# State space phase: x scaled by 1/rms as it is turned, B loaded ahead of w_in, u and z copied out by ScalarE, drive of the states behind two projections

## Chip, cores, metric

One core of a Trainium2 chip. The metric is the device time of one execution in microseconds (us), median of three runs. PE is TensorE, DVE VectorE, ACT ScalarE, POOL GpSimd, SP SyncE (it issues the DMAs here).

## What is computed

x is 256 tokens by 1024 columns. Two layers follow: an S5 mixer and an attention mixer, then two blocks of feed forward and hybrid mixer. The change touches the S5 mixer alone:

```python
def rms_norm(x, g):
    y = xf * lax.rsqrt(jnp.mean(xf * xf, axis=-1, keepdims=True) + NORM_EPS)
    return (y * g).astype(x.dtype)

def s5_mixer(h, w_in, a_re, a_im, log_dt, b_re, b_im, c_re, c_im, d_skip, w_glu, b_glu, w_out):
    proj = h @ w_in
    u, z = proj[..., :SSM_WIDTH], proj[..., SSM_WIDTH:]
    ...   # dt, ab = exp(a*dt), f = (ab - 1)/a, all complex; bu = B u per group of 16 channels
    ...   # s[t] = ab * s[t-1] + f * bu[t], by an associative scan over 256 tokens
    y = Re(C s) + d_skip * uf
    y = jax.nn.gelu(y)
    y = y * jax.nn.sigmoid(y @ w_glu + b_glu)
    y = y * jax.nn.silu(z)
    return y @ w_out
```

There are 64 groups of 16 channels with 64 complex states each.

## The kernel before

All engines run the program in the order in which it is written (a manual schedule), so the order of the source lines in `ssm` is the order on each engine; SP issues loads in their written order, and a load waits until its buffer is free.

Tiling. Channels lie on partitions, 8 blocks of 128 (`KC`). Tokens are cut into 64 chunks (`J`) of 4 (`L`). Two groups share a partition axis of 128 states, so there are 32 pairs (`NPR`). Within a chunk the work is matrix products: `vt` (B times powers of a, turned) carries u into the state increment of a chunk (`drive`), `kt` carries u of a chunk to y of the same chunk (`within`), `cp` (C times powers of a) reads states into y (`read`). Between chunks the states `S` are scanned on DVE in levels: `pre4` and `pre8` join chunks in twos and fours, `chain` takes 16 steps in a row over the fours, `post8` and `post4` fill in the rest. `drive(0)` and `drive(1)` each make half of the pairs; `settle` copies them from PSUM to S, one half on ACT and one on DVE; p4[0], p4[1], p8[0], p8[1] are the levels of the first half of the pairs, p4[2], p4[3], p8[2], p8[3] those of the second.

Projection. x is turned by 16 PE transposes (L772), ACT copies it out times the gain g (L779) to `xg`, and `proj(s)` (L790) makes 256 of the 2048 columns of w_in: s = 0 to 3 are u, 4 to 7 are z. 1/rms of a token isn't in xg: `norm()` finds it on DVE, PE spreads it over the partitions (L339), DVE copies it to `R` (rstd, L1154), and `evac_u` and `gate` on DVE multiply it in as they copy u and z out of PSUM with tokens regrouped as (t, j):

```python
    def evac_u(s):
        for m in range(2):
            V.tensor_tensor(u[:, 2 * s + m], perm(us[s][:, m]), perm(R), op=ALU.mult)
```

Parameters. `powers()` on DVE makes the powers of a from a_re, a_im and log_dt; `cmul` is a complex product of B or C (`raw`, tile `bc`) with one of them; `spread` (ACT, L976) lays a result out as `bx` (for B) or `cp` (for C); `turn_c` turns C on PE (L951) and ACT copies it back (L956); `turn_b` turns bx (L994), ACT copies it to vt (L997). `kernels` (L1062) makes `kps` on PE, `turn_k` (L1069) copies it turned to `kt`. `rest1` (L2092, L2094) turns bias rows on PE (`rows`) and copies them on DVE (`cols`).

The order around the change is: turns of x, proj(0); powers; B products woven with norm(); proj(1), proj(2); u(0), u(1), u(2) copied out; proj(3) woven with turn_b; drive(0) between its halves; p4[0], p4[1], p8[0]; u(3); kernels; drive(1); proj(4), proj(5); then DVE's p4[2] to p8[3]; turn_k woven with the first steps of chain; rest1; proj(6), proj(7); within; chain woven with gate(4), gate(5); post levels with four reads; then the GLU products with w_glu (L1261).

Of the kernel before, what the change touches and what calls it, by code (L numbers as in the profile page):

```python
# [18 lines left out]
P = 128  # L19
# [684 lines left out]
L = 4  # L704
# [4 lines left out]
def ssm(K, x, g, gcol, w_in, a_re, a_im, log_dt, b_re, b_im, c_re, c_im, d_skip, w_glu, rest0, rest1, rest2, w_out, follow):  # L709
# [21 lines left out]
    nc.sync.dma_start(h[:, 1], x[P:T])  # L731
    w0 = K.wp.tile([P, KC, 256], F32, tag="raw", name=K.name("raw"), bufs=3)
# [35 lines left out]
    xg = K.e([P, KC, T], "xg")  # L768
    xps = [K.psum("acc" if 0 < k < 3 else "ps", [P, 2, 2, P], "xp") for k in range(4)]
    for t in range(2):  # L770
        for k in range(KC):
            nc.tensor.transpose(xps[k // 2][:, k % 2, t], h[:, t, k * P:(k + 1) * P], K.ident)  # L772
        if t == 0:
            gp = K.psum("acc", [P, 2 * KC], "gp")
            nc.tensor.transpose(gp, g16, K.ident[:2 * KC, :2 * KC])
            nc.scalar.copy(gcol.rearrange("p l m -> p (l m)"), gp)
    xps = [x.rearrange("p i t c -> p i (t c)") for x in xps]
    for k in range(KC):
        nc.scalar.activation(xg[:, k], xps[k // 2][:, k % 2], AF.Copy, scale=gcol[:, 0, k:k + 1])  # L779
# [23 lines left out]

    run(proj(0))
# [79 lines left out]
    def powers():  # L884
        run(expm1(dt, t2))
        V.tensor_copy(pr[:, 0:2], pt)
        stt(dt, em, 1.0, t2, ALU.add, ALU.mult)
        tt(mag, lr, dt)
        tt(th, li, dt)
        for _ in zip_longest(magnitude(), trig()):  # L890
            pass
        tt(t1, t5, sn)
        tt(t2, sn, sn)
        tt(ai, t1, mag)
        stt(cm, t2, -2.0, mag, ALU.mult, ALU.mult)
        tt(ar, mag, cm, ALU.add)
# [82 lines left out]
    def perm(ap):  # L979
        return ap.rearrange("p (j t) -> p t j", t=L)  # L980
# [56 lines left out]
    def pre4(b):  # L1037
        return level(b, 1, slice(2, None, 2), slice(1, None, 2))
# [93 lines left out]
    wr, wh, wl = [], [], []  # L1132
    load()
    spread(lambda b: bx[b][:, :, 3], bp[3])
    nc.scalar.copy(cin[:, :, :, 1], cin[:, :, :, 0])
    nm = norm()
    run(weave(cmul(bp[2], bp[3], ar, ai), nm, 3))
    run(nm)
    run(proj(1))
    load()  # L1140
    rp = K.rows(stat[0], 2)
    R = K.ap.tile([P, T], F32, tag="rstd", name=K.name("rstd"), bufs=2)
    spread(lambda b: bx[b][:, :, 2], bp[2])
    run(cmul(bp[1], bp[2], ar, ai))
    spread(lambda b: bx[b][:, :, 1], bp[1])
    evacs = [turn_c(0, 0), turn_c(0, 4), turn_c(1, 0)]
    run(proj(2))
    for f in evacs:
        f()
    evacs = turn_c(1, 4)  # L1150
    run(cmul(bp[0], bp[1], ar, ai))
    spread(lambda b: bx[b][:, :, 0], bp[0])
    evacs()
    V.tensor_copy(R, rp)  # L1154
    evac_u(0)
    evac_u(1)
    factors()
    squarings()
    load()
    evac_u(2)  # L1160
# [8 lines left out]
    p3 = proj(3)  # L1169
    cp = [K.wp.tile([P, 2, L, 8, 2 * CH], F32, tag="wlo", name=K.name("cp")) for _ in range(4)]  # L1170

    def later(t):
        run(cmul(nxt, cur, ar, nai1))
        spread(lambda b: cp[b][:, :, t], nxt)
        return nxt, cur

# [5 lines left out]
    for m in range(4):  # L1182
        run(turn_b(m))
        run(p3, 2)
    cur, nxt = later(0)
    cur, nxt = later(1)
# [23 lines left out]
    skip = K.t([P, KC, 2 * CH], "skip")  # L1210
    V.tensor_tensor(skip, K.eye32[:, None, :].broadcast_to([P, KC, 2 * CH]),
                    dsk[:, :, None].broadcast_to([P, KC, 2 * CH]), op=ALU.mult)
    kt = K.e([P, KC, L, 2 * CH], "kt")
# [12 lines left out]
    for s in (4, 5):  # L1226
        run(weave(gate(s), ch))
# [16 lines left out]
    for s in (6, 7):  # L1244
        run(gate(s))
# [6 lines left out]
    for s in range(4, 8):  # L1252
        silu(s)
# [916 lines left out]
```

## Time and profile before

| | us |
|---|---|
| median of 3 runs (1393.80 to 1394.67) | 1394.28 |
| the profiled execution, its own time | 1394.2 |
| its span in the profile | 1392.1 |
| PE busy, share of the span | 1360.4, 98% |
| DVE busy | 1101.1, 79% |
| ACT busy | 817.5, 59% |
| first GLU product, the end of the stretch that the change touches | 125.96 |

Times in the profile are us from the span's start. In a row of the timeline the first number is the start, the second the time to the end of the group, then engine, line, operation, tiles written and read, shapes, and how many; in square brackets is how long the engine stood idle before and what ended that. An fp32 matmul counts as two PE instructions, a transpose as one. PE's ends are modelled; the distance from start to start is the surer measure.

### The profile page before, as it was taken

Reading aid. Unit: us, or ns where it says so; the run is one execution under the profiler, and the core shown is the slowest. Engines: PE = TensorE matmul, PEld = TensorE weight load, DVE = VectorE, ACT = ScalarE, POOL = GpSimd, SP = SyncE. Lnnn points to the kernel's source line nnn. Section 1 sums busy time; section 2 is a strip of 40 time slices with the busy share of each in tenths; the row PEclk is TensorE's granted clock in tenths of the full one; section 3 lists DMA queues with packets and bytes.
Section 4 is the critical chain, followed back from the end, with each engine's and each line's share of the span. In section 5 each row is a group of like instructions: output and inputs, shape, how many; then the busy total and the mean of one; then the engine's idle time right before and its main releaser. Section 6 shows DMA issues by size and latency. Waiting matters only on the chain. (4 is left out here: it accounts for less than half of the span.)

```text
span 1392.1 us, 21232 instructions
## 1 busy us (share of the span) xinstructions
PE 1360.4 (98%) x8205; PEld 1148.8 (83%) x8205; DVE 1101.1 (79%) x1801; ACT 817.5 (59%) x1589; POOL 27.4 (2%) x35
## 2 busy tenths in 40 slices
PE   8988999999999999999999999999999999999996
PEld 7877888987888899887878888788899887878885
DVE  8889788678996589777799747998469987698954
ACT  6524667665765484565676546666457564656642
POOL 0003100000000000000000000000000000000000
PEclk9999999999999999999999999999999999999998
DMA  8233655366637444455844656365535445747350
GB/s 217 63 112 119 207 172 170 123 189 234 222 111 241 150 155 159 152 165 168 272 137 166 198 188 222 125 236 182 199 128 187 138 163 177 225 150 259 119 183 30
DMA packets 181348, 237.17 MB, mean 170 GB/s; under 512 B 16952, under 2 KB 140144, under 8 KB 181248
## 3 DMA queue, kind: packets, MB, share of 16 engines
q1 hardware_dynamic: 180160, 233.47, 51.5%
q0 software_dynamic: 672, 1.81, 0.4%
q8 instruction: 64, 1.05, 0.3%
q10 hardware_dynamic: 416, 0.55, 0.1%
q14 instruction: 36, 0.29, 0.1%
HBM read 234.76 MB, written 1.05 MB: 169 GB/s over the span
## 5 line engine op out<-in xcount | busy, mean ns | idle before, releaser
L191 ACT CAST whi<-raw 128x512 fp32r<-128x512 f32 x688 | 379.2, 620 | 137.5 <-PE p L289 87.3
L203 DVE TENSOR_TENSOR wlo<-raw,whi 128x1024 fp32r<-128x1024 f32 x344 | 407.4, 1217 | 7.8 <-ACT whi L191 7.4
L287 PE MATMUL p<-whi,xghi 128*128 128x512 f32 x800 | 320.5, 401 | 0.0
L289 PE MATMUL p<-whi,xglo 128*128 128x512 f32 x800 | 312.5, 391 | 0.0
L288 PE MATMUL p<-wlo,xghi 128*128 128x512 f32 x800 | 311.8, 390 | 0.0
L289 PEld LDWEIGHTS p<-whi,xglo 128*128 128x128 f32 x800 | 150.1, 188 | 32.4
L288 PEld LDWEIGHTS p<-wlo,xghi 128*128 128x128 f32 x800 | 150.6, 188 | 28.7
L287 PEld LDWEIGHTS p<-whi,xghi 128*128 128x128 f32 x800 | 150.4, 188 | 28.6
L191 ACT CAST whi<-quad 128x512 fp32r<-128x512 f32 x192 | 106.5, 618 | 60.7 <-DVE quad L168 27.8
L287 PE MATMUL acc<-whi,hh 128*128 128x512 f32 x352 | 141.7, 402 | 0.0
L288 PE MATMUL acc<-wlo,hh 128*128 128x512 f32 x352 | 138.7, 394 | 0.1
L289 PE MATMUL acc<-whi,hh 128*128 128x512 f32 x352 | 138.1, 392 | 0.0
L203 DVE TENSOR_TENSOR wlo<-quad,whi 128x1024 fp32r<-128x1024 f32 x96 | 114.3, 1217 | 0.0
L506 DVE SCALAR_TENSOR_TENSOR hid<-p,col,hid 128x256 f32<-128x256 f32 x64 | 30.8, 481 | 75.5 <-ACT hid L505 75.1
L288 PEld LDWEIGHTS acc<-wlo,hh 128*128 128x128 f32 x352 | 66.2, 188 | 15.7 <-DVE wlo L203 3.8
L289 PEld LDWEIGHTS acc<-whi,hh 128*128 128x128 f32 x352 | 66.1, 188 | 15.4 <-DVE hh L301 1.7
L287 PEld LDWEIGHTS acc<-whi,hh 128*128 128x128 f32 x352 | 66.1, 188 | 13.7 <-ACT hh L300 1.6
L287 PE MATMUL g<-xghi,whi 128*128 128x256 f32 x256 | 73.8, 288 | 0.0
L289 PE MATMUL g<-xghi,wlo 128*128 128x256 f32 x256 | 72.4, 283 | 0.0
L288 PE MATMUL g<-xglo,whi 128*128 128x256 f32 x256 | 72.4, 283 | 0.0
L301 DVE TENSOR_TENSOR hh<-tph,hh 128x512 fp32r<-128x512 f32 x44 | 30.4, 690 | 49.6 <-ACT hh L300 49.3
L790 PE MATMUL g<-xg,raw 128*128 128x256 f32 x256 | 60.3, 392 | 4.6 <-DVE kt L1069 3.6
(375 smaller groups left out, 2248.6 us busy)
## 6 DMA issues: line engine op xcount, KB each, us to landing
raw<-in_ffn_w_down_dram SPq DMA_DIRECT2D x44, 1024.0 KB, 5.0
raw<-in_w_in_dram SPq DMA_DIRECT2D x36, 1024.0 KB, 5.1
raw<-in_ffn_w_gate_dram SPq DMA_DIRECT2D x56, 512.0 KB, 4.1
raw<-in_ffn_w_up_dram SPq DMA_DIRECT2D x56, 512.0 KB, 5.1
raw<-in_attn_w_in_dram SPq DMA_DIRECT2D x16, 1024.0 KB, 5.6
quad<-in_ffn_w_gate_dram SPq DMA_DIRECT2D x32, 512.0 KB, 8.8
quad<-in_ffn_w_up_dram SPq DMA_DIRECT2D x32, 512.0 KB, 8.8
raw<-in_w_out_dram SPq DMA_DIRECT2D x8, 1024.0 KB, 5.3
```

What stands on the lines that cost most here:

```text
L191: self.nc.scalar.copy(hf[:, sl], raw[:, sl])
L203: self.nc.vector.tensor_tensor(out, raw, hi.bitcast(F32), op=ALU.subtract)
L287: nc.tensor.matmul(out, ah, bh, start=start, stop=False, skip_group_check=more)
L288: nc.tensor.matmul(out, ah, bl, start=False, stop=False, skip_group_check=more)
L289: nc.tensor.matmul(out, al, bh, start=False, stop=stop, skip_group_check=more)
L301: self.nc.vector.tensor_tensor(lo, x, hi.bitcast(F32), op=ALU.subtract)
L506: V.scalar_tensor_tensor(hid[j, t], s[:, 256:512], norm.col05[:, t:t + 1], a, op0=ALU.mult, op1=ALU.mult)
L790: nc.tensor.matmul(us[s][:, m], ws[s][:, k, m * P:(m + 1) * P], xg[:, k], start=k == 0, stop=k == KC - 1)
```

## The change

x is turned by products with a diagonal matrix `dg` that holds 1/rms, so xg already has it; R, its spread and its copy are gone. u and z (4, 5) are copied out by ACT without a product, z (6, 7) goes through silu straight from PSUM. norm() stands inside powers() from its seventh turn on. B is loaded ahead of w0. proj(0) stands behind powers, C's turns behind proj(0) and proj(1), turn_b(0) to (3) and drive(0) behind these two; proj(2) and proj(3) follow drive(0) whole. turn_k, skip and the settling of the second half stand right behind drive(1), p8[1] ahead of it, the last spread of cp behind it. The chain is woven with nothing.

```diff
+    raw = K.e([P, 2, 2, NPR, CH], "bc")
+    for i, b in enumerate((b_re, b_im)):
+        nc.sync.dma_start(raw[:, 0, i], ...)
     w0 = ...
-    for t in range(2):
-        for k in range(KC):
-            nc.tensor.transpose(xps[k // 2][:, k % 2, t], h[:, t, k * P:(k + 1) * P], K.ident)
...
-    run(proj(0))
...
-        for _ in zip_longest(magnitude(), trig()):
-            pass
+        nm = norm()
+        for i, _ in enumerate(zip_longest(magnitude(), trig())):
+            if i >= 6:
+                next(nm, None)
+        run(nm)
...
     def evac_u(s):
-        for m in range(2):
-            V.tensor_tensor(u[:, 2 * s + m], perm(us[s][:, m]), perm(R), op=ALU.mult)
+        nc.scalar.copy(u[:, 2 * s:2 * s + 2], us[s].rearrange("p m (j t) -> p m t j", t=L))
...
     def gate(s):
-        for m in range(2):
-            V.tensor_tensor(z[:, 2 * (s - 4) + m], perm(us[s][:, m]), perm(R), op=ALU.mult)
-            yield
+        nc.scalar.copy(z[:, 2 * (s - 4):2 * (s - 4) + 2], us[s].rearrange("p m (j t) -> p m t j", t=L))
...
+    spread(lambda b: bx[b][:, :, 3], bp[3])
+    for t in range(2):
+        V.tensor_scalar(dg[:, t], K.ident, stat[0][:, t:t + 1], None, op0=ALU.mult)
...
+    for k in range(KC):
+        for t in range(2):
+            nc.tensor.matmul(xps[k // 2][:, k % 2, t], h[:, t, k * P:(k + 1) * P], dg[:, t], start=True, stop=True)
+        nc.scalar.activation(xg[:, k], xps[k // 2][:, k % 2].rearrange("p t c -> p (t c)"), AF.Copy,
+                             scale=gcol[:, 0, k:k + 1])
     load()
+    run(cmul(bp[2], bp[3], ar, ai))
+    run(proj(0))
...
+    evac_u(1)
+    for m in range(4):
+        run(turn_b(m))
+        if m == 0:
+            for f in evacs:
+                f()
     factors()
     squarings()
...
+    cur, nxt = later()
+    vq = drive(0)
+    laid(0)
+    cur, nxt = later()
+    settled(0, vq)
+    laid(1)
+    run(proj(2))
     load()
+    evac_u(2)
     run(p4[0])
     run(weave(p4[1], p8[0]))
+    run(p8[1])
+    run(proj(3))
     evac_u(3)
+    for m in range(4, KC):
+        run(turn_b(m))
     kps = [kernels(hf) for hf in range(2)]
+    cur, nxt = later()
+    laid(2)
+    later()
     vq = drive(1)
+    for hf in range(2):
+        run(turn_k(hf))
     settled(1, vq)
+    laid(3)
     run(proj(4))
-    run(weave(p4[2], p8[1]))
+    run(p4[2])
     run(weave(p4[3], p8[2]))
     run(p8[3])
     run(proj(5))
     ch = chain()
-    for hf in range(2):
-        run(weave(turn_k(hf), ch))
     b_glu = rest1(rowsin)
     run(proj(6))
...
     for s in (4, 5):
-        run(weave(gate(s), ch))
+        gate(s)
     run(ch)
```

On PE from the parameters' transposes (pt) on, before: xp is x turned, gp the gains, g a projection.

```order
L763 MATMUL pt_121<-ident,prm_76 128x32 x2
L772 MATMUL xp_131<-ident,h 128x128 x2
L772 MATMUL xp_132<-ident,h 128x128 x2
L772 MATMUL xp_133<-ident,h 128x128 x2
L772 MATMUL xp_134<-ident,h 128x128 x2
L775 MATMUL gp_143<-ident,norm_g_rows_82 128x16
```

The same place in the change, with the first turn of C (ct) and the second projection:

```order
L763 MATMUL pt_121<-ident,prm_76 128x32 x2
L1123 MATMUL gp_232<-ident,norm_g_rows_82 128x16
L1127 MATMUL xp_228<-dg_224,h 128x128 x4
L1127 MATMUL xp_229<-dg_224,h 128x128 x4
L1127 MATMUL xp_230<-dg_224,h 128x128 x4
L1127 MATMUL xp_231<-dg_224,h 128x128 x4
L778 MATMUL g_267<-xg_227,raw_88 128x256 x16
L940 MATMUL ct_299<-ident,cin_93 128x128 x4
L940 MATMUL ct_304<-ident,cin_93 128x128 x4
L778 MATMUL g_324<-xg_227,raw_91 128x256 x16
L940 MATMUL ct_349<-ident,cin_93 128x128 x4
```

The turns of x now read dg, which DVE makes, and the first turns of C stand between the two projections. On PE behind the last product of drive(0) (vq), before: proj(3) in pieces of two, with turns of B (vp) between.

```order
L1020 MATMUL vq_544<-u_246,vt_248 128x64
L790 MATMUL g_468<-xg_130,raw_251 128x256 x2
L994 MATMUL vp_683<-ident,bx_110 128x128 x4
L994 MATMUL vp_689<-ident,bx_110 128x128 x4
L790 MATMUL g_468<-xg_130,raw_251 128x256 x2
```

The same place in the change:

```order
L1005 MATMUL vq_490<-u_211,vt_213 128x64
L778 MATMUL g_649<-xg_227,raw_96 128x256 x16
L778 MATMUL g_693<-xg_227,raw_259 128x256 x16
L979 MATMUL vp_711<-ident,bx_110 128x128 x4
L979 MATMUL vp_717<-ident,bx_110 128x128 x4
```

Two whole projections stand there now. On DVE at the copy of the bias columns (cols), before: four steps of the chain (m, S), and the turns of the kernels (kt), stand ahead of it.

```order
L1071 TENSOR_TENSOR kt_1063<-kt_1063,skip_1061 128x4x32
L1005 TENSOR_TENSOR m_1080<-S_114,apow_184 128x64
L1006 TENSOR_TENSOR m_1081<-S_114,apow_184 128x64
L1007 TENSOR_TENSOR m_1080<-m_1080,S_114 128x64
L1009 TENSOR_TENSOR S_114<-m_1080,m_1081 128x64
L2094 COPY cols<-rows_1086 128x72
L1109 TENSOR_TENSOR z_1260<-g_993,rstd_304 128x256
```

The same place in the change, where p8[3] is ahead and the whole chain behind:

```order
L992 TENSOR_TENSOR m_1037<-m_1037,S_114 128x256
L994 TENSOR_TENSOR S_114<-m_1037,m_1038 128x2x8x16
L2094 COPY cols<-rows_1062 128x72
L990 TENSOR_TENSOR m_1239<-S_114,apow_135 128x64
L991 TENSOR_TENSOR m_1240<-S_114,apow_135 128x64
```

The copy moved from behind the fourth step of the chain to ahead of the first; on PE `rows` stands behind proj(5) in both.

## Rows read from the trace of the kernel before

**Rows 1.** Busy time by stretch: length, PE, PEld, DVE, ACT, POOL, granted clock, DMA share, GB/s

```profile
5.50:9.40 3.90, 3.84 (x17) 3.47 (x18) 3.73 (x33) 1.11 (x4) 0.00 (x0) 1.00 1.11 340
86.40:89.70 3.30, 3.16 (x8) 2.52 (x9) 3.23 (x17) 1.11 (x1) 0.00 (x0) 0.50 0.30 107
126.00:1390.00 1264.00, 1250.29 (x6437) 1052.08 (x6436) 990.57 (x1480) 759.30 (x1466) 22.80 (x24) 1.00 0.54 176
```

**Rows 2.** Waits, 0 to 140 us: engine, line, for whom: total, times, longest

```profile
PE yps L1090 <- DVE S L1009: 4.1, 3, 2.2
...
PE g L790 <- DVE kt L1069: 3.6, 1, 3.6
```

**Rows 3.** Timeline of DVE, 53 to 104 us

```profile
53.89 0.69 DVE L1005 TENSOR_TENSOR m<-S,apow 128x512 f32<-128x512 f32 x1
...
56.43 0.68 DVE L1005 TENSOR_TENSOR m<-S,apow 128x512 f32<-128x512 f32 x1
...
73.02 1.42 DVE L1027 COPY S<-vq 128x256 f32<-128x256 f32 x4 [3.63 <-ACT S L1029]
...
78.92 0.69 DVE L1005 TENSOR_TENSOR m<-S,apow 128x512 f32<-128x512 f32 x1
...
85.44 0.42 DVE L1211 TENSOR_TENSOR skip<-eye,dsk 128x256 f32<-128x256 f32 x1
...
97.02 0.28 DVE L1009 TENSOR_TENSOR S<-m,m 128x64 f32<-128x64 f32 x1
...
97.99 0.27 DVE L1009 TENSOR_TENSOR S<-m,m 128x64 f32<-128x64 f32 x1
...
103.92 0.61 DVE L1005 TENSOR_TENSOR m<-S,apow 128x256 f32<-128x256 f32 x1
```

**Rows 4.** Timeline of PE, 0 to 126 us

```profile
5.56 1.97 PE L772 MATMUL xp<-ident,h 128*128 128x128 f32 x8 [1.91 <-DMA h<-in_x_dram]
...
9.43 7.98 PE L790 MATMUL g<-xg,raw 128*128 128x256 f32 x32
...
36.26 1.04 PE L994 MATMUL vp<-ident,bx 128*128 128x128 f32 x8
37.13 1.03 PE L790 MATMUL g<-xg,raw 128*128 128x256 f32 x4
...
41.57 7.37 PE L1020 MATMUL vq<-u,vt 32*128 32x64 f32 x256
...
57.80 3.77 PE L1062 MATMUL kps<-bx,cx 128*32 128x128 f32 x128
61.51 7.37 PE L1020 MATMUL vq<-u,vt 32*128 32x64 f32 x256
68.81 14.08 PE L790 MATMUL g<-xg,raw 128*128 128x256 f32 x64
82.73 0.23 PE L2092 MATMUL rows<-ident,rowsin 72*128 72x72 f32 x1
86.54 15.66 PE L790 MATMUL g<-xg,raw 128*128 128x256 f32 x64 [3.58 <-DVE kt L1069]
102.12 8.90 PE L1080 MATMUL yps<-u,kt 32*32 32x256 f32 x256
...
125.96 3.14 PE L1261 MATMUL g<-yhi,whi 128*128 128x256 f32 x24
```

**Rows 5.** Timeline of ACT, 14 to 143 us

```profile
14.58 3.30 ACT L976 ACTIVATE bx<-bc,own 128x256 f32<-128x256 f32 x8 [1.02 <-DMA bc<-in_ssm_b_im_dram]
...
28.06 2.33 ACT L956 ACTIVATE bc<-ct 64x256 f32<-64x256 f32 x6
...
53.10 2.05 ACT L997 COPY vt<-vp 128x512 f32<-128x512 f32 x4
...
140.54 2.12 ACT L300 CAST ohi<-gl 128x512 fp32r<-128x512 f32 x2
```

**Rows 6.** Timeline of DVE, the last step of powers

```profile
11.63 0.19 DVE L822 TENSOR_TENSOR pr<-pr 128x32 f32<-128x32 f32 x1
```

More of the change, by code (lines that the diff above doesn't have):

```diff
@@ L767, in ssm @@
     nc.scalar.copy(warm, K.ones)
-    xg = K.e([P, KC, T], "xg")
-    xps = [K.psum("acc" if 0 < k < 3 else "ps", [P, 2, 2, P], "xp") for k in range(4)]
-    for t in range(2):
-        for k in range(KC):
-            nc.tensor.transpose(xps[k // 2][:, k % 2, t], h[:, t, k * P:(k + 1) * P], K.ident)
[L773 to L779, printed above, removed]
     ss = K.s([P, 2], "ss")
@@ L1132, in ssm @@
     wr, wh, wl = [], [], []
+    spread(lambda b: bx[b][:, :, 3], bp[3])
+    dg = K.t([P, 2, P], "dg")
+    for t in range(2):
+        V.tensor_scalar(dg[:, t], K.ident, stat[0][:, t:t + 1], None, op0=ALU.mult)
+    xg = K.e([P, KC, T], "xg")
+    xps = [K.psum("acc" if 0 < k < 3 else "ps", [P, 2, 2, P], "xp") for k in range(4)]
+    gp = K.psum("acc", [P, 2 * KC], "gp")
+    nc.tensor.transpose(gp, g16, K.ident[:2 * KC, :2 * KC])
+    nc.scalar.copy(gcol.rearrange("p l m -> p (l m)"), gp)
+    for k in range(KC):
[3 more added lines that the diff above has]
+                             scale=gcol[:, 0, k:k + 1])
     load()
-    spread(lambda b: bx[b][:, :, 3], bp[3])
+    run(cmul(bp[2], bp[3], ar, ai))
+    run(proj(0))
+    spread(lambda b: bx[b][:, :, 2], bp[2])
     nc.scalar.copy(cin[:, :, :, 1], cin[:, :, :, 0])
-    nm = norm()
-    run(weave(cmul(bp[2], bp[3], ar, ai), nm, 3))
-    run(nm)
+    run(cmul(bp[1], bp[2], ar, ai))
+    evacs = [turn_c(0, 0), turn_c(0, 4)]
+    evac_u(0)
+    load()
+    for f in evacs:
+        f()
+    spread(lambda b: bx[b][:, :, 1], bp[1])
     run(proj(1))
     load()
[L1141 to L1150, printed above, removed]
     run(cmul(bp[0], bp[1], ar, ai))
+    evacs = [turn_c(1, 0), turn_c(1, 4)]
     spread(lambda b: bx[b][:, :, 0], bp[0])
-    evacs()
-    V.tensor_copy(R, rp)
-    evac_u(0)
     evac_u(1)
+    for m in range(4):
+        run(turn_b(m))
+        if m == 0:
+            for f in evacs:
+                f()
     factors()
     squarings()
-    load()
-    evac_u(2)
     cur, nxt = raw[:, 1], raw[:, 0]
@@ L1168, in ssm, with later, laid @@
                             op0=ALU.mult)
-    p3 = proj(3)
     cp = [K.wp.tile([P, 2, L, 8, 2 * CH], F32, tag="wlo", name=K.name("cp")) for _ in range(4)]
-    def later(t):
+    def later():
         run(cmul(nxt, cur, ar, nai1))
-        spread(lambda b: cp[b][:, :, t], nxt)
         return nxt, cur
+    def laid(t):
+        spread(lambda b: cp[b][:, :, t], cur)
     def settled(hf, vq):
@@ L1180, in settled @@
                 settle(hf, vq, q, i)
[L1182 to L1186, printed above, removed]
+    cur, nxt = later()
     vq = drive(0)
+    laid(0)
+    cur, nxt = later()
     settled(0, vq)
-    for m in range(4, KC):
-        run(p3, 2)
-        run(turn_b(m))
+    laid(1)
+    run(proj(2))
     load()
+    evac_u(2)
     p4 = [pre4(b) for b in range(4)]
@@ L1196, in ssm @@
     run(weave(p4[1], p8[0]))
+    run(p8[1])
+    run(proj(3))
     evac_u(3)
+    for m in range(4, KC):
+        run(turn_b(m))
     kps = [kernels(hf) for hf in range(2)]
+    cur, nxt = later()
+    laid(2)
+    later()
+    cur, nxt = nxt, cur
     vq = drive(1)
-    cur, nxt = later(2)
-    later(3)
+    skip = K.t([P, KC, 2 * CH], "skip")
+    V.tensor_tensor(skip, K.eye32[:, None, :].broadcast_to([P, KC, 2 * CH]),
+                    dsk[:, :, None].broadcast_to([P, KC, 2 * CH]), op=ALU.mult)
+    kt = K.e([P, KC, L, 2 * CH], "kt")
+    for hf in range(2):
+        run(turn_k(hf))
     settled(1, vq)
+    laid(3)
     run(proj(4))
     load()
-    run(weave(p4[2], p8[1]))
+    run(p4[2])
     run(weave(p4[3], p8[2]))
@@ L1209, in ssm @@
     unit_raw()
[L1210 to L1213, printed above, removed]
     ch = chain()
-    for hf in range(2):
-        run(weave(turn_k(hf), ch))
     b_glu = rest1(rowsin)
@@ L1244, in ssm @@
     for s in (6, 7):
-        run(gate(s))
+        silu(s)
     for b in range(2):
@@ L1251, in ssm @@
     unit_low()
-    for s in range(4, 8):
+    for s in range(4, 6):
         silu(s)
```

8 lines of the change are left out of this document (2 added, 6 removed).

## Prediction

> **What bounds the kernel now.** I read the busy time by stretch first: from 126 us to the end PE is busy 1250 of 1264 us [rows 1], so whatever delays or advances the first gate product (125.96, the GLU's first matmul) passes to the end one for one. The question is when that product starts. Up to there the waits of PE [rows 2] name two things: 3.6 us for the transposed read-out kernels `kt` ahead of proj(6), and 4.1 us in front of three of the four state reads, for DVE. Behind the first the clock fell: PE stood still until 86.54 and then had 0.50 (1.2 GHz) granted up to 89.7 [rows 1, 4]. So the end of this phase hangs on DVE's chain of states. One step of it takes 0.97 us (97.02 to 97.99), its sixteen steps end at 103.92 [rows 3], and the gate product follows 22.0 us later. That chain in turn hangs on drive(1), behind which proj(4) starts at 68.81 [rows 4]; I call that time X. Before, X to the end of the chain is 35.1 us.
>
> **The turn of x, and proj(0).** Sixteen transposes of h become sixteen fp32 products of h with diag(1/rms), which cannot start before 1/rms exists. DVE ended `powers` at 11.82 [rows 6]. Eleven small steps of norm() go into it: eight between independent steps, three in a row at the end. Each costs between nothing and 0.19 (that row); I take 0.13, 1.4 in all, and 0.3 for the two diagonals: the first product at 13.5, where PE before began at 5.56.
> A proj is 6.96 us (13.92 for two, 68.81 to 82.73 [rows 4]) for 16 products of 256 columns, 0.435 each, so 0.22 for 128 columns: 3.5 us for the turn at full clock, 7.0 at half. Which one? Eight transposes took 1.97 at 5.56 and 1.04 at 36.26 [rows 4], and proj(0) took 7.98 instead of 6.96, which a slow stretch of 2.0 us would do: until 11.4 PE ran at half speed, 5.9 us after it took up work. After 86.54 it was 3.2 us [rows 1]. Ahead of 13.5 PE stands nearly idle again, so I take 4.5 us at half speed: ten products, then six at 0.22. The turn ends at 19.2 (18.5 with 3.2 us, 19.8 with 5.9). The granted-clock row of 5.5 to 9.4 says 1.00 all the same [rows 1]; by it the turn would end at 17.0. The Trainium skill (TensorE: Matmul & The Clock Gate, section "What's actually happening") has the array's clock throttled by default until activity releases it; by that rule the end is again 19.2 and not 17.0, and the durations agree.
> ACT's side is covered: B lands at the latest when it did (14.58 [rows 5]), since it now stands ahead of w0; 3.3 of spread and eight copies of xg by 21.0 at the latest, and proj(0) wants the last xg only 3 us after its start. w0 behind B costs nothing as long as it lands by 19, and before it was needed at 9.43. So proj(0) runs from 19.2 to E = 26.2; before it began at 9.43.
>
> **From E to drive(0).** Here ACT is the longest, since it now copies u too and everything stands behind proj(0)'s copy. Prices [rows 5]: a 128x512 copy out of PSUM 0.5 (four in 2.05), a copy of turned C 0.39 (six in 2.33), a spread 3.3. In its order: u(0), then C waits for eight transposes (0.87, 36.26 to 37.13 [rows 4]) and ends at E+2.65; two spreads, E+9.2; u(1) 0.5; the first two vt copies 1.0; four copies of C 1.55; six vt copies 3.0 and 0.2 for the two turns between. Sum E+15.5: drive(0) starts at 41.7. PE alone needs 12.2 (proj(1) 6.96, 48 transposes 5.2), so it waits 3.3 us there. Before, drive(0) started at 41.57 [rows 4] with proj(2) and half of proj(3) already done.
>
> **From drive(0) to X.** This is all PE: drive 7.3, proj(2) and proj(3) 13.9, the turns of B 3.5, kernels 3.7 (57.80 to 61.51), drive(1) 7.3 [rows 4]. Sum 35.7, so X = 77.4, 8.6 later than before. DVE keeps up: settle, p4[0], p4[1] and two p8 are some 11 us of that time (by the like rows below), and two complex products and kt follow.
>
> **DVE behind X.** u, z and the copy of R leave DVE, kt and one p8 move ahead of X. What remains: settle, 1.42 and some 0.5 for its release (73.02 row), p4[2] 2.54 (53.89 to 56.43), p4[3] with p8[2] and p8[3] 6.52 (78.92 to 85.44) [rows 3]: ready at X+11.0 = 88.4. But the next instruction on DVE is now the copy of `cols`, and its transposition `rows` stands on PE behind proj(4) and proj(5): X+13.92+0.23 = 91.6. **This is a new wait of 3.4 us with the whole chain queued behind it.** Before, the copy stood four steps into the chain and `rows` was long done (82.73). The Trainium skill (Perfetto Trace Analysis, section "Tensor Engine Instruction") calls DVE a strict FIFO; if a step could pass the waiting copy, the chain would start at 88.5, which is the second rival. No row of before shows such a passing.
> So the chain starts at 91.8, takes 16 x 0.97 = 15.5, and ends at 107.3: 3.4 later than 103.92. From 85.44 to 103.92 it had 18.5 with skip, kt, cols and four gates woven in. PE is not late: X + 13.9 + 0.3 + 13.9 + 8.8 (102.12 row) = 114.4, where the first read becomes ready too. proj(6) no longer waits 3.6 for kt, but that time is spent waiting for DVE at the reads. Behind the last state the gates 6 and 7 leave DVE; PE had other products there, so nothing is gained. ACT's gates 4 and 5 and silu from PSUM stand where it is idle.
>
> **Sum.** 3.4 us, and 0.4 for two costs that the trace does not show. The copies of u read PSUM with a stride: 0.5 as the vt copies, or 1.06 as the strided ohi casts (two in 2.12 [rows 5]); three stand on the path, so 0 to 1.7. I stay near 0.5, because ohi writes with a stride and u reads with one. And PE is little busy before drive(0); if the clock falls as at 86.4, up to 3.4 us at half speed cost up to 1.7. The profiled run took 1394.2 (median 1394.28, so the same): **1398.0 us.**
>
> **Rivals.**
> First, not slower: the turn of x at full clock, or the ramp over early. Then proj(0) starts at 17.0 and all moves 2.2: 1395.8. For it: the granted-clock row; against it: transposes at half rate. It decides at a start of proj(0) before 18.2, where the loss falls under 2.8 us. Chance 0.22.
> Second, the cols copy doesn't hold the chain: chain from 88.5 to 104.0, last read as before, ahead of which PE, at 114.4, still has time for the first three: 1394.7. Against it: the order of DVE. Chance 0.07.
> Third, the tail of ACT: strided copies at 1.06 and drive(0) half cold, +3.3: 1401.3. Chance 0.18.
> Fourth, first and second together: 1392.5; a gain over 2.8 us needs half a microsecond more still, from a shorter ACT stretch. Chance 0.08.
>
> **How the numbers follow.** The forecast (1396.8 to 1399.8) has 0.45. About 0.2% (2.8 us) is what a measurement tells from no change. Slower: 0.45 and 0.18 but for an edge, so 0.60. Same: 0.22, 0.07 and that edge, 0.32. Faster 0.08. The range 1394.6 to 1401.6 leaves out the fourth case and parts of the second and third.
>
> **What would show it.** In the changed kernel: first product of h with the diagonal at 13.5, proj(0) at 19.2; drive(0) at 41.7 with ACT's vt copy as releaser; proj(4) at 77.4; DVE idle some 3.4 us ahead of the cols copy, released by PE `rows`; no wait ahead of proj(6); sixteen steps of 0.97 ending at 107.3; gate product at 129.4. Wrong I am if proj(0) starts before 18, if drive(0) starts at 40 or earlier, or if the cols copy finds its rows ready.

## The result and the profile after

The changed kernel takes 1404.36 us (median of four executions, 1403.6 to 1404.73), the kernel before 1394.29 beside it: 1.0071 times as long, 95% interval 1.0056 to 1.0086, **10.1 us slower**. The forecast was 1398.0, at most 1401.6: the sign was right, nearly two thirds of the loss were missed. The profiled execution took 1404.73 with a span of 1402.2. In the kernels below whose products for the turn of x run without pauses, some executions take 3 to 9 us more than the others, at a mean clock of 0.989 to 0.995 instead of 0.994 to 0.998; the four of these that were profiled grant 0.50 in drive(0) or right behind it, while the changed kernel had none in its four.

From the first GLU product on nothing changed: 1264.2 us from 135.8 to 1400, with PE busy for 1250.6 of them, as in [rows 1]. So the loss lies ahead of that product, which starts at 135.77 instead of 125.96 [rows 4].

Stretch from 135.8 us, columns as in [rows 1]:

```profile
135.80:1400.00 1264.20, 1250.60 (x6438) 1052.14 (x6436) 989.75 (x1479) 759.13 (x1466) 15.35 (x24) 1.00 0.54 176
```

Timeline of PE up to there (start, length, engine, line, operation, tiles, count, idle time ahead of it and its releaser):

```profile
13.16 1.22 PE L1127 MATMUL xp<-dg,h 128*128 128x128 f32 x4 [7.85 <-DVE dg L1119]
15.89 2.08 PE L1127 MATMUL xp<-dg,h 128*128 128x128 f32 x8 [1.51 <-ACT xg L1128]
18.53 2.08 PE L1127 MATMUL xp<-dg,h 128*128 128x128 f32 x8 [0.56 <-ACT xg L1128]
...
24.83 9.50 PE L778 MATMUL g<-xg,raw 128*128 128x256 f32 x32
34.17 1.04 PE L940 MATMUL ct<-ident,cin 128*128 128x128 f32 x8
...
47.72 8.72 PE L1005 MATMUL vq<-u,vt 32*128 32x64 f32 x256
56.38 14.08 PE L778 MATMUL g<-xg,raw 128*128 128x256 f32 x64
...
84.89 14.08 PE L778 MATMUL g<-xg,raw 128*128 128x256 f32 x64
98.80 0.23 PE L2092 MATMUL rows<-ident,rowsin 72*128 72x72 f32 x1
```

The new thing is in the first lines. Inside the turn of x, PE waits for ACT's copy `xg`, once 1.51 us and three times 0.56, and two k take 2.64 (15.89 to 18.53). ACT's own rows show the other half of the same circle: each second copy waits 1.31 for PE. The first wait of PE is the longest because ACT still works on the spread of B until 15.28. (The last row is a copy of u, of use further down.)

```profile
11.97 3.31 ACT L965 ACTIVATE bx<-bc,own 128x256 f32<-128x256 f32 x8 [3.64 <-DMA bc<-in_ssm_b_im_dram]
...
15.37 0.47 ACT L1128 ACTIVATE xg<-xp,norm_g 128x256 f32<-128x256 f32 x1
17.15 0.47 ACT L1128 ACTIVATE xg<-xp,norm_g 128x256 f32<-128x256 f32 x1 [1.31 <-PE xp L1127]
...
34.37 0.59 ACT L971 COPY u<-g 128x512 f32<-128x512 f32 x1 [4.70 <-PE g L778]
```

The code says why. One PSUM tile `xp` holds two k, and the copy of k is written between the products of k and those of k+1. For even k the products of k+1 write the other half of the tile which that copy reads, and they wait until it is done. Behind them proj(0) still runs at half speed for half of its length: 14 records in 4.9 us, then 23 in 4.5 (the stretches 24.8 to 29.7 and 29.7 to 34.2; a record on an edge counts in both).

```profile
24.80:29.70 4.90, 4.90 (x14) 3.91 (x13) 4.07 (x38) 4.59 (x10) 0.00 (x0) 1.00 0.00 1
29.70:34.20 4.50, 4.50 (x23) 3.91 (x22) 0.00 (x0) 0.00 (x0) 0.00 (x0) 1.00 0.00 0
```

Further down the trace looks as forecast. DVE's copy of `cols` waits 2.94 us for `rows`, with the chain queued behind it:

```profile
99.07 0.23 DVE L2094 COPY cols<-rows 128x72 f32<-128x72 f32 x1 [2.94 <-PE rows L2092]
99.22 0.26 DVE L990 TENSOR_TENSOR m<-S,apow 128x64 f32<-128x64 f32 x1
```

### The profile page after: what moved, and what is told of

Same layout as the page of the kernel before. It is cut to its first block, busy times and chain, and to the rows that moved or that the text cites. A ratio compares the mean times of both kernels' runs of the same rounds, so it can differ in the third digit from the quotient of the medians.

```text
span 1402.2 us, 21244 instructions
## 1 busy us (share of the span) xinstructions
PE 1364.8 (97%) x8217; PEld 1152.0 (82%) x8217; DVE 1093.9 (78%) x1786; ACT 820.9 (59%) x1595; POOL 19.9 (1%) x35
## 4 chain that ended last, share of the span: by engine, by line
PE 89%; DVE 6%; ACT 3%; DMA 1%; issue 1%; SPq 0%; DVEq 0%; ACTq 0%
PE p L287 17%; PE p L289 16%; PE p L288 16%; PE acc L288 6%; PE acc L289 6%; PE acc L287 6%; PE g L778 4%; PE g L288 2%; PE g L287 2%; PE g L289 2%; DVE wlo L203 2%; PE tph L512 1%; PE lv L1738 1%; PE vq L1005 1%; PE tp L376 1%
```

## The experiments

Theory 1: the alternation of products and copies over one tile costs what was missed, directly (the waits) and through the clock, which stays low while PE keeps pausing. Rivals: the cold clock by itself; `rows`; ACT, B or the place of drive(0). Unless said otherwise, edits are made to the changed kernel with all products of the turn ahead of all copies ("products in a row").

### Products in a row

```diff
     for k in range(KC):
         for t in range(2):
             nc.tensor.matmul(xps[k // 2][:, k % 2, t], h[:, t, k * P:(k + 1) * P], dg[:, t], start=True, stop=True)
+    for k in range(KC):
         nc.scalar.activation(xg[:, k], xps[k // 2][:, k % 2].rearrange("p t c -> p (t c)"), AF.Copy,
```

> The changed kernel with one edit: all sixteen products of h with the diagonal are written first, then the eight copies to xg (in the change copy k stands between the products of k and k+1, and two k share one PSUM tile). Theory 1, the alternation: PE waits four times for ACT only because product k+1 goes into the tile that copy k reads; without it the products run back to back from 13.2, end at or before 20.2 (sixteen of 0.435 at half clock), and PE, no longer pausing, has its full clock back sooner than at 29.7: proj(0) begins at 19 to 20 instead of 24.8 and ends near 27 instead of 34.2. 1397.3 us, between 1396 and 1399. Rival, the clock alone (the slow stretch explains all of it and the waits cost nothing by themselves): sixteen slow products and a slow proj(0) are as long as before, less than 2 us gained, 1403 us.

Measured: 1396.32, 1.0024 (1.0007 to 1.0042) of before; 8.0 less than the changed kernel. Eight of ten executions took 1395.6 to 1397.7, two 1405. PE's timeline:

```profile
12.96 5.54 PE L1127 MATMUL xp<-dg,h 128*128 128x128 f32 x32 [8.03 <-DVE dg L1119]
18.34 7.07 PE L778 MATMUL g<-xg,raw 128*128 128x256 f32 x32
...
38.80 8.73 PE L1005 MATMUL vq<-u,vt 32*128 32x64 f32 x256
...
75.97 14.08 PE L778 MATMUL g<-xg,raw 128*128 128x256 f32 x64
...
127.17 3.01 PE L1262 MATMUL g<-yhi,whi 128*128 128x256 f32 x23
```

No wait inside the turn, and X and the first GLU product 8.9 and 8.6 earlier than in the changed kernel. Of the 8.9 the four waits are 3.2 (1.51 and three of 0.56); some 5.5 is speed: the products themselves take 3.1 less (5.38 for the turn, against 11.67 less the waits), and proj(0) 2.4 less (6.91 against 9.34). This is the kernel that the prediction had described. Theory 1 stands; whether order or tile does it, the next run tells.

### Alternating by tile

```diff
-    for k in range(KC):
-        for t in range(2):
+    for k in range(0, KC, 2):
+        for j in (k, k + 1):
+            for t in range(2):
...
+        for j in (k, k + 1):
+            nc.scalar.activation(xg[:, j], xps[j // 2][:, j % 2].rearrange("p t c -> p (t c)"), AF.Copy,
```

> The changed kernel with the turn of x written by PSUM tile: the four products of k and k+1, then their two copies. Products and copies still alternate, but no product shares a tile with a copy written ahead of it. Theory 1 (the products of odd k wait because the copy of k-1 reads the tile that they write): PE doesn't wait for ACT within the turn, proj(0) starts at 18.3 and X lies at 76.0, as with all products first; 1396.3. Rival (products and copies written in turn hold each other up, whatever the tile): proj(0) stays near 24.8, X at 84.9, 1404.

Measured: five of ten executions 1395.9 to 1397.0, the others 1402.9 to 1406.1; 1.0037 (1.0016 to 1.0057) over all. The trace is one of the others:

```profile
12.97 6.74 PE L1128 MATMUL xp<-dg,h 128*128 128x128 f32 x32 [8.32 <-DVE dg L1119]
19.55 7.07 PE L778 MATMUL g<-xg,raw 128*128 128x256 f32 x32
...
40.01 13.86 PE L1005 MATMUL vq<-u,vt 32*128 32x64 f32 x256
```

Products and copies still alternate, yet PE doesn't wait: it is the shared tile, not the alternation. The turn takes 6.6 instead of 5.4, without a wait, so at half speed for longer; that, drive(0) at half clock (13.86 instead of 8.73) and 1.4 in the projections behind it make up this execution's time.

### The clock by itself

In the changed kernel, with products and copies as there:

```diff
+    for _ in range(24):
+        nc.tensor.matmul(xps[3][:, 1, 1], K.ident, K.ident, start=True, stop=True)
     nc.tensor.transpose(gp, g16, K.ident[:2 * KC, :2 * KC])
```

> The changed kernel with 24 products of the identity with itself added on PE between the parameters' transposes and the gains' transpose, so that PE is busy while it would wait for the diagonals; their output is written over. Theory 1 (alternation and half speed both cost): at full clock a pair of k takes 1.8 instead of 2.64, the turn ends near 21.7, proj(0) takes 7.0: E at 28.7 instead of 34.2, 1398.9 us. Rival, the alternation alone with the copies as the pace: only proj(0) gets shorter by 2.4, 1402 us. Rival, the clock is not raised by such products: no change, 1404 us.

Measured: 1403.67, 1.0055 (1.0035 to 1.0076). The first four records take 0.71 instead of 1.22, so the clock was up at 13.12; then PE waits for the copies as before, and 0.50 is granted:

```profile
13.12 0.71 PE L1129 MATMUL xp<-dg,h 128*128 128x128 f32 x4 [1.50 <-DVE dg L1119]
15.41 2.08 PE L1129 MATMUL xp<-dg,h 128*128 128x128 f32 x8 [1.58 <-ACT xg L1130]
```

```profile
14.70:28.40 13.70, 11.29 (x38) 9.60 (x39) 13.53 (x50) 7.29 (x19) 0.00 (x0) 0.50 0.71 183
```

So warming alone didn't undo the loss in this execution. One of the four took 1398.38 with a mean clock of 0.997, close to the 1398.9 of theory 1; it has no trace. What the pauses inside the turn do shows beside the run of all three edits (below), with the same 24 products, a pause of 2.11 us behind them and none in the turn. There, too, 0.50 was granted, but for 3.4 us instead of 13.7:

```profile
13.70:17.00 3.30, 3.30 (x18) 3.30 (x17) 3.23 (x5) 2.77 (x8) 0.00 (x0) 0.50 1.02 339
```

So the clock can fall behind the pause ahead of the turn alone, and with further pauses in the turn it stayed low longer. The three traces with the waits in the turn agree: proj(0) took 8.3 to 9.5, while behind a turn without waits it took 7.1 in every trace.

### Rows early, and all three together

In the changed kernel the transposition `rows` goes ahead of proj(1) and the copy of `cols` behind squarings():

```diff
     evacs = [turn_c(0, 0), turn_c(0, 4)]
+    turned = rest1(rowsin)
...
     squarings()
+    b_glu = rest1(rowsin, turned)
...
-    b_glu = rest1(rowsin)
     run(proj(6))
```

> The changed kernel with one edit: the bias rows are turned on PE right behind the first turns of C, and copied to cols on DVE behind the squarings, where DVE stands idle; nothing else waits for them. Theory: the 2.9 us that DVE waits ahead of the chain are on the path, so the chain starts at 96.1 instead of 99.2 and the first gate product comes 2.9 earlier: 1401.5 us. Rival, PE is as late as DVE there (within ends at 121.7, four reads behind it): less than 1 us gained, 1403.7 us.

> All three edits together in the changed kernel (products first, rows early, 24 warming products). Theory 1 with the wait for cols on the path: proj(0) begins when the copies of xg allow it, near 17, and ends at 24 instead of 34.2; ten us earlier, and 2.9 from the rows: 1391.5 us, under the kernel before. Rival, that ACT's stretch up to drive(0) or DVE takes over once PE is early: 1395 us or more.

Measured: 1402.02, 1.0056 (1.0041 to 1.0071); all three together (products in a row, warming, early rows) 1396.41, 1.0022 (1.0007 to 1.0037), no better than the products in a row alone: the turn ends as late, at 18.32, with 0.50 granted from 13.7 to 17.1. With early rows alone the total is 2.3 less than in the changed kernel, near theory's 1401.5, but not for theory's reason. The wait of 2.94 is gone, yet X to the first GLU product is 50.66 instead of 50.88 (83.44 to 134.10). In the trace 1.45 of the gain lies ahead of X, most of it in proj(0), which is ahead of the edit and left half speed sooner. PE's timeline (proj(0), then the reads), then the last step of DVE that a read needs:

```profile
24.43 8.34 PE L778 MATMUL g<-xg,raw 128*128 128x256 f32 x32
...
129.52 1.99 PE L1075 MATMUL yps<-S,cp 128*32 128x64 f32 x128 [2.01 <-issue]
133.52 0.65 PE L1075 MATMUL yps<-S,cp 128*32 128x64 f32 x29 [2.01 <-issue]
134.10 2.17 PE L1262 MATMUL g<-yhi,whi 128*128 128x256 f32 x16
```

```profile
128.25 0.69 DVE L994 TENSOR_TENSOR S<-m,m 128x512 f32<-128x512 f32 x1
```

The states were ready at 128.94, and the last stretch of reads began at 133.52, with PE waiting for nothing that the profile shows ("issue"). The `cols` wait is real and about as long as foretold, but it stood in front of a second limit, so removing it is worth little: 0.2, and 0.6 between the run of all three (50.63) and the products in a row alone (51.20), of which some 0.3 is half clock in the last reads of the latter (0.50 from 122.4 to 125.8).

### The other parts, one by one

B behind w0 again, u by VectorE, and proj(2) ahead of the turns of B (products in a row in all):

```diff
     ws.append(w0)
+    raw = K.e([P, 2, 2, NPR, CH], "bc")
+    for i, b in enumerate((b_re, b_im)):
+        nc.sync.dma_start(raw[:, 0, i], b.rearrange("(q g) p c -> (g p) q c", g=2))
```

> Products in a row, and B loaded behind w0 again, as in the kernel before. Theory (what the load order earns is the spread of B ahead of the xg copies on ACT): the spread starts at 14 to 14.6 instead of 11.5, ends near 17.8, the first xg copy starts there instead of 14.9, proj(0) starts at 20.5 to 21 instead of 18.34, X = 78.3, 1398.5 to 1399. Rival (the copies of xg have slack, and w0 was what came late): proj(0) stays within 0.5 us of 18.34 and the time within 1 us of 1396.3.

```diff
-        nc.scalar.copy(u[:, 2 * s:2 * s + 2], us[s].rearrange("p m (j t) -> p m t j", t=L))
+        V.tensor_copy(u[:, 2 * s:2 * s + 2], us[s].rearrange("p m (j t) -> p m t j", t=L))
```

> Products in a row, and the four copies of u by VectorE instead of ScalarE (z stays with ScalarE). Theory 1 (from proj(0)'s end to drive(0) ACT is the longest): two copies of 0.59 leave it, drive(0) lasts 7.5 instead of 8.73 and ends 1.2 us earlier, X = 74.8, and the first GLU product 126.0; DVE has 8.4 us idle ahead of the read-outs of C and 5.8 ahead of settle, which take the copies. 1395.1. Rival (DVE's copy comes late behind its complex products, or PE bounds that stretch): X stays at 76.0 or becomes later, 1396.3 to 1397.

```diff
     evac_u(1)
+    for f in evacs:
+        f()
+    run(proj(2))
     for m in range(4):
         run(turn_b(m))
...
     laid(1)
-    run(proj(2))
```

> Products in a row, and proj(2) ahead of the turns of B and of drive(0) (the place of drive(0) right behind two projections is undone; the copies of C go ahead of it). In the run without the alternation PE loses 0.24 us ahead of drive(0) and 1.36 within it (8.73 instead of 7.37), since ACT's vt copies come late. Theory 1 (X is the sum of PE's work from proj(0) on, plus these waits): drive(0) lasts 7.3 to 7.4, X = 74.4, 1.6 earlier, and the first GLU product 125.6 or a little later; 1394.7. Rival (the place of drive(0) is what earns time, since DVE's settle and steps of hf 0 get a start): DVE is late, the cols copy no longer waits for rows but DVE arrives later than X+14, and the time is 1396.3 or more.

Measured. **B late:** 1396.44, 1.0024 (1.0009 to 1.004; two of ten above 1402), the rival. ACT's spread does start at 14.63 and the copies of xg at 18.02, but the copies come every 0.38 us and proj(0) takes them one by one, so it starts at 18.72, where the turn ends. With products in a row the load order earns nothing.

```profile
14.63 3.30 ACT L965 ACTIVATE bx<-bc,own 128x256 f32<-128x256 f32 x8 [6.89 <-DMA bc<-in_ssm_b_im_dram]
...
18.02 3.03 ACT L1129 ACTIVATE xg<-xp,norm_g 128x256 f32<-128x256 f32 x8
```

**u by VectorE:** 1398.59, 1.0037 (1.002 to 1.0054), slower. drive(0) doesn't gain (38.70, 8.72 long), and behind it PE waits for a copy of u that comes late on DVE: X at 77.70 instead of 75.97.

```profile
65.05 1.53 PE L979 MATMUL vp<-ident,bx 128*128 128x128 f32 x12 [1.36 <-DVE u L971]
```

So the copies by ScalarE are worth 1.7 us at X. **proj(2) early:** five of ten executions 1394.5 to 1395.7, the other five 1400.4 to 1402.2; 1.0025 over all. The profiled one is of the latter (drive(0) 12.83, at half clock), so its X says nothing on theory 1.

### Without the wait for 1/rms

The spread of B goes behind the copies of xg here, too.

```diff
-            nc.tensor.matmul(xps[k // 2][:, k % 2, t], h[:, t, k * P:(k + 1) * P], dg[:, t], start=True, stop=True)
+            nc.tensor.matmul(xps[k // 2][:, k % 2, t], h[:, t, k * P:(k + 1) * P], K.ident, start=True, stop=True)
```

> Products in a row, against the identity instead of diag(1/rms), and the spread of B behind the xg copies: this leaves out the factor 1/rms, so that the turn needn't wait for it. It prices that wait. Theory (the wait for 1/rms is what the change pays; E to X is the same 50.7 as in the run with the products in a row, 25.25 to 75.97): the turn starts at 5.5, w0, which lands behind B, lets proj(0) start near 13 instead of 18.34, E is at 20 to 20.5, X at 71 to 72, first GLU product at 122 to 123, 1391 to 1392. Rival (ACT with its spreads and copies, or B, holds drive(0) where it is): E comes earlier, but drive(0) stays at 38.8 and X at 76; 1396.3.

Measured: seven of ten executions 1391.5 to 1393.6, three at 1400; 0.9999 (0.9982 to 1.0016) over all.

```profile
13.67 7.15 PE L778 MATMUL g<-xg,raw 128*128 128x256 f32 x32 [1.55 <-DMA raw<-in_ssm_w_in_dram]
...
72.53 14.08 PE L778 MATMUL g<-xg,raw 128*128 128x256 f32 x64
...
123.36 3.13 PE L1259 MATMUL g<-yhi,whi 128*128 128x256 f32 x24
```

The first GLU product comes 3.8 earlier than with products in a row. That is what the wait for 1/rms still costs, up to where w0, landing behind B, takes over. In this execution, the fastest of the ten, the rest of the change is 2.6 ahead of before (125.96); over all ten, three of them at 1400, it is no faster.

### Early transposes, with the order of the change

1/rms back into VectorE's copies of u and z; transposes, proj(0) and loads as before; then the order of the change, once with only that, once with proj(2) woven between the turns of B, once with proj(1) ahead of the turns of C as well. The copy of u in all three:

```diff
-        nc.scalar.copy(u[:, 2 * s:2 * s + 2], us[s].rearrange("p m (j t) -> p m t j", t=L))
+        for m in range(2):
+            V.tensor_tensor(u[:, 2 * s + m], perm(us[s][:, m]), perm(R), op=ALU.mult)
```

> The change without its first two parts and without its third: the transposes of h, proj(0) and the load order stand where the kernel before has them, and u and z are multiplied by 1/rms in VectorE's copies, as there; the order behind proj(0) is that of the change (drive behind two projections, kt, skip and one p8 ahead of proj(4)). Theory 1 (the order alone: ACT's work bounds drive(0)): B lands at 14.6, and from there 4 spreads of 3.3, 1.0 for cin, 8 copies of C of 0.39 and 8 of vt of 0.5 end at 36; drive(0) ends at 43.5 to 44, and 28.5 of PE work behind it and 1.4 for late copies of u put X at 72 to 73.5. First GLU product 51 to 53 later, 123.5 to 126.5; 1392 to 1395. Rival (PE bounds: nothing gained from an earlier E): X below 70, 1390 or less. Third: DVE, with u and z back, becomes the bound, X + 55 and more: 1396 and above.

> The same, with proj(2) woven between the four turns of B ahead of drive(0), four products ahead of each turn. Theory 1 (PE stands still behind proj(1) while ACT spreads; proj(2) fills that time): drive(0) at 36 to 38, and behind it only proj(3), the turns of B, kernels and drive(1), 21.5: X at 66 to 68, ahead of before's 68.81; behind it 51 to 54 to the first GLU product, 117 to 122 (before 125.96): 1385 to 1390, faster than both kernels. Rival (DVE, with u and z to copy and settle(0) later, is late for the chain): X + 58, as before, and 1394.

> The transposes of h, proj(0), the load order and the factor 1/rms in VectorE's copies as in the kernel before, with the order of the change behind, and mended where the run with early transposes lost its time: proj(1) stands ahead of the turns of C on PE (there the turns of C waited 7.9 us for ACT with proj(1) behind them), and half of proj(2) ahead of the turns of B, the rest between them. Theory 1 (the order of the change is worth its time where PE needn't wait for 1/rms): ACT ends its spreads, copies of C and vt at 36 to 37, drive(0) at 37 to 38, X at 66 to 67 (before 68.81), and 53 behind it, as in the run with early transposes, the first GLU product: 119 to 120; 1387 to 1389, faster than both kernels. Rival (DVE is late for the chain with u, z and 1/rms back on it): X as said, but 57 to 58 behind it as in the kernel before; 1393. Third (the clock falls on the way, as in the trace with early transposes): 3 to 5 us more than by theory 1.

Measured: 1403.2, 1403.49 and 1402.25, 1.0074, 1.0059 and 1.0045 of before (1.0031 to 1.006 in the last). All theories on them fell. In the first two the turns of C wait 7.93 us for ACT, and 0.50 is granted for ten us, from within that wait on; in the third X is at 79.72, since PE waits 2.74 for ACT's vt behind drive(0), and the clock falls in drive(0). No run here shows the order of the change paying where VectorE applies 1/rms; whether a better placing would was not tried further.

```profile
25.54 1.97 PE L953 MATMUL ct<-ident,cin 128*128 128x128 f32 x8 [7.93 <-ACT cin L1141]
```

```profile
64.72 4.07 PE L996 MATMUL vp<-ident,bx 128*128 128x128 f32 x20 [2.74 <-ACT vt L999]
```

### What lets the clock fall in drive(0)

proj(2) right ahead of drive(0) (products in a row), and proj(2) woven between the turns of B:

```diff
     cur, nxt = later()
+    run(proj(2))
     vq = drive(0)
...
     laid(1)
-    run(proj(2))
```

> Products of the turn in a row, and proj(2) between the turns of B and drive(0). In the traces where drive(0) met half the clock (granted 0.50 for 13.7 us, X 7 to 8 us later) it stands right behind 4 to 5 us of turns. Theory 1 (that stretch of small products is why the clock falls): behind 6.9 us of full products drive(0) keeps the clock in all runs; it also finds all its vt, so that it lasts 7.37 instead of 8.73; X at 74.4 to 74.6, first GLU product 125.6 to 126; 1394.7 to 1395.2, and no run near 1403. Rival (the clock's fall doesn't hang on what stands just ahead of drive(0)): some runs are 6 to 8 us above the others, as in the other kernels of this family.

> Products of the turn in a row, and proj(2) woven between the turns of B, four products ahead of each turn, as the kernel before weaves proj(3) there. Theory 1 (that small products in a row ahead of drive(0) let the clock fall): no run near 1403; drive(0) waits less for vt (7.4 to 8), X at 74.4 to 75, 1394.7 to 1395.5. Rival: some runs are 6 to 8 us above the others; the rest as said.

Measured: 1395.49, 1.0003 (0.9993 to 1.0012), with nine of ten between 1393.75 and 1396.3, one at 1398.55 and none near 1403; X comes only 0.4 earlier than with products in a row. Woven: 1397.82, 1.0016 (1.0001 to 1.0032), five of seven at 1397 to 1402. The trace of the first (start of turns, proj(2), drive(0), X), then a stretch of the second, behind drive(0)'s middle:

```profile
35.48 3.69 PE L979 MATMUL vp<-ident,bx 128*128 128x128 f32 x24 [0.24 <-ACT vt L982]
39.01 7.07 PE L778 MATMUL g<-xg,raw 128*128 128x256 f32 x32
46.01 4.91 PE L1005 MATMUL vq<-u,vt 32*128 32x64 f32 x167
51.34 2.69 PE L1005 MATMUL vq<-u,vt 32*128 32x64 f32 x89 [0.42 <-issue]
...
75.56 14.08 PE L778 MATMUL g<-xg,raw 128*128 128x256 f32 x64
```

```profile
52.30:59.10 6.80, 6.80 (x73) 5.98 (x67) 3.22 (x7) 3.66 (x11) 0.00 (x0) 0.50 0.01 2
```

With a whole projection right ahead of drive(0) no execution went above 1399.3, here or in the two kernels below that have it (33 in all); with pieces of it between the turns, or all of it ahead of them, some took 1400 to 1402. The clock isn't safe even so: a trace below has 0.50 right behind drive(0). Why is open. drive(1), which follows 7.3 us of small records, ran at full clock in these traces. But right ahead of it stand 3.7 us of products (`kps`), right ahead of drive(0), with products in a row, only transposes of C and B; no run tells whether that decides.

### A clock that is up in time

Products in a row, 35 products of the identity ahead of the turn, B's spread behind the copies of xg; then 31 of them, proj(2) right ahead of drive(0) and early rows; then the same without early rows, where the edits are these two:

```diff
+    for _ in range(31):
+        nc.tensor.matmul(xps[3][:, 1, 1], K.ident, K.ident, start=True, stop=True)
     nc.tensor.transpose(gp, g16, K.ident[:2 * KC, :2 * KC])
...
+    run(proj(2))
     vq = drive(0)
```

> All products of the turn in a row, as in the run that undid the alternation (proj(0) from 18.34 us, X = 75.97, first GLU product 127.17, 1396.3 us); the spread of B behind the xg copies instead of ahead of them; and 35 products of the identity ahead of the transposed gains, so that PE works without a pause until the first product of h. Theory 1 (the turn is slow because of the clock: 5.4 us for sixteen products that take 3.5 at full clock, and PE stood still before them): granted clock 1.00 from 8 us on, proj(0) starts at 16.7, X = 74.4, first GLU product 125.3 to 125.6, 1394.5 to 1395. Rival (the products are paced by something else, the copies or the loads of h as weights): proj(0) stays at 18.3, 1396.3.

> What the runs point to, together: products of the turn in a row, proj(2) right ahead of drive(0), the transposition `rows` and the copy `cols` early, and 31 products of the identity ahead of the transposed gains, so that PE works until close to the first product of h. Theory 1: the turn runs at full clock for most of its length, proj(0) starts at 16.8 to 17.5 instead of 18.64, X at 73.8 to 74.5 instead of 75.56, and 50.6 behind it the first GLU product at 124.4 to 125.1 (before 125.96, products in a row and proj(2) late 126.20): 1393 to 1394, at most 0.1% ahead of the kernel before. Rival (the clock falls again in the pause between the identities and the turn, as with 24 of them): proj(0) at 18.3 or later, the first GLU product at 126, 1395; some runs 1398 and more.

> The run before without the early `rows`: there the turn ran at full clock and proj(0) started at 16.76, but `rows` then stood ahead of proj(1) on PE and waited 1.43 us for its input (proj(1) at 26.23, as late as without the gain). Theory 1: proj(1) starts at 24.6, X at 73.7 to 74 instead of 75.56 to 75.83, the first GLU product 50.7 later at 124.3 to 124.8 (before 125.96): 1393.0 to 1393.7, 0.1% ahead of the kernel before. Rival (ACT's spreads of B bound drive(0), whatever E): X stays at 75.5, the first GLU product at 126.2, 1394.8.

Measured. With 35 the turn takes 3.84 instead of 5.54, at full clock: theory 1 on the turn holds. But the identities end 1.7 late, so proj(0) starts at 18.36 all the same, and the moved spread holds the turns of C for 1.33. Six of ten executions took some 8 us more than the other four, the profiled one in and behind drive(0): 1403.7, 1.004 (1.0021 to 1.006).

```profile
14.68 3.84 PE L1128 MATMUL xp<-dg,h 128*128 128x128 f32 x32
```

```profile
43.70:57.40 13.70, 13.70 (x199) 12.87 (x196) 11.59 (x20) 7.22 (x20) 0.00 (x0) 0.50 0.01 2
```

With 31 and early rows: 1394.76, 1.0001 (0.9992 to 1.001). proj(0) starts at 16.76, but `rows` now holds proj(1) for its input. Without early rows: **1393.31, 0.9981 (0.9972 to 0.999): 0.2% faster than before** (1395.67 beside it) and faster than the change, and all eleven executions within 1392.4 to 1394.8. PE's timelines, the one with early rows first:

```profile
16.76 7.07 PE L778 MATMUL g<-xg,raw 128*128 128x256 f32 x32
...
26.14 0.26 PE L2097 MATMUL rows<-ident,rowsin 72*128 72x72 f32 x1 [1.43 <-DMA rowsin<-in_hgrn_norm_dram]
```

```profile
12.95 3.84 PE L1129 MATMUL xp<-dg,h 128*128 128x128 f32 x32
16.63 7.07 PE L778 MATMUL g<-xg,raw 128*128 128x256 f32 x32
...
44.00 6.79 PE L1005 MATMUL vq<-u,vt 32*128 32x64 f32 x233
51.47 0.97 PE L1005 MATMUL vq<-u,vt 32*128 32x64 f32 x23 [0.67 <-issue]
52.37 8.74 PE L778 MATMUL g<-xg,raw 128*128 128x256 f32 x32
```

```profile
52.30:55.50 3.20, 3.20 (x10) 2.52 (x8) 2.84 (x7) 3.20 (x10) 0.00 (x0) 0.50 0.02 5
```

drive(0) starts at 44.00 instead of 46.01, so the earlier turn passes through. This profiled execution (1394.77) is the slowest of the eleven: it gave the 2.0 back, 0.4 in drive(0) and 1.6 behind it (proj(3) 8.74 instead of 7.17, at half clock), so its X is 75.54, its first GLU product 126.58. That the faster ten kept the 2 us to the end is read from their times alone; they have no trace.

## Why the prediction was wrong, point by point

**The turn of x, and proj(0): this step failed.** It took the turn to be sixteen products in a row. The start was right (13.5; 13.16), the turn was 5.7 and measured 11.67 (13.16 to 24.83), proj(0) was 6.96 and measured 9.34, so E came at 34.17, 8.0 late. The step put ACT's copies down as covered, since proj(0) needs the last one late; it never asked whether a *product* waits for a copy, and so put that wait at nothing. It was 3.2 us in itself, and the rest of the 8 is the half speed that lasted through it. The order of PE and ACT side by side, with the tile numbers, would have shown it: two k in one tile, a copy of it between their products. With products in a row the turn took 5.38 and proj(0) started at 18.34, against 19.2 foretold.

**The clock: half speed right, its length wrong.** Half speed at the start of the turn was right, and the durations, not the granted-clock row, told it, as the first rival was weighed. The 4.5 us of it assumed that PE keeps working; without waits it was 3.5 (13 to 16.5). In the changed kernel, where PE paused every 2.64, it lasted until 29.7, by the records in proj(0).

**From E to drive(0).** Foretold E+15.5, measured E+13.55, but PE then waits inside for the vt copies (8.72 instead of 7.3): drive(0) ends at E+22.2 against 22.8. Right within 0.6. ACT's strided copies of u cost 0.59, the vt copies 0.59 to 0.69; the third rival's price of 1.06 fell.

**From drive(0) to X.** 28.5 (56.38 to 84.89), foretold 28.4. **DVE behind X.** The wait for `rows` is 2.94 against 3.4 (the prediction's own times, 88.4 and 91.6, give 3.2), X to the first GLU product 50.9 against 52.0; proj(6) no longer waits, as said. What failed is the price: the second rival gave 3.3 for the chain without that wait, the run with early rows 0.2. No step passed the waiting copy. That DVE works in strict order, as the prediction cites from the Trainium skill (Perfetto Trace Analysis, section "Tensor Engine Instruction"), agrees with the row.

**The sum.** 8.0 (turn and proj(0)), less 0.6, plus 0.1, less 1.1, is 6.4 at the first GLU product (135.77 against 129.4). It leaves some 0.3 of the 6.7 by which the forecast missed the profiled execution. The kernel with products in a row, for which every other step was worked out, took 1396.3 and lay inside the range, 1.7 under the forecast: foretold E 26.2, X 77.4, product 129.4, measured 25.25, 75.97, 127.17. And the chances: all four rivals varied the clock or waits that the text had found; none was a new wait inside a part that the change writes anew. None of the three signs of being wrong showed, either: they looked for a start of proj(0) that is too early, not for one that is late.

## What to carry to other kernels

Where two engines alternate over a PSUM tile, count the dependency per tile, not per slice: write all writers of a tile ahead of its first reader. A loop that makes PE pause can pay twice, once for the wait and once for the clock (here 3.2 and some 5.5 us). And when a queue's wait is removed, look for the limit right behind it before booking the gain: here the early `rows` removed a wait of 2.9 us and gained 0.2 to 0.6.

## What the runs showed of the hardware

- The granted clock read 1.00 from 13 to 16.5 us with products in a row, while 16 records took 3.5 us and the next 18 took 1.8 (16.5 to 18.3): there the durations have to be read, not that column.
- After 24 products of the identity PE stood still for 1.50 us, worked on two products (four records), stood still for 1.58 and then three times for 0.56, and 0.50 was granted from 14.7 to 28.4. With one pause of 2.11 us and none behind it, it was granted from 13.7 to 17.1; with a pause of 0.30 us or none, not at all in the turn.
- The clock also fell while PE was busy throughout: 0.50 from 43.7 to 57.4, in drive(0) and behind it, in one trace, and not at all there in those of three kernels with the same order on PE from proj(0) on (products in a row, B late, u by VectorE). What decides it wasn't found.
- Streams of small products (128 records of 64 columns, 1.99 us) stood still for 1.46 to 2.01 us at a time in the run with early rows, with no releaser in the profile; for the last of these pauses the states had been ready since 128.94. The instruction queue moved five packets, 0.08 MB, in the 24 us around them; that it causes the pauses was not tested.
- A copy that reads PSUM with a stride (u, 128x512) took 0.59 us on ACT, no more than one that reads it in order (vt, 0.59 to 0.69).
